# A mixture of experts after two transformer blocks: gather and output combination as two rounded passes instead of one fp32 product

## The chip, the cores and the metric

The program runs on one core of a Trainium2 chip as one launch. The metric is the device time in microseconds (us), taken from the outside. The profile comes from one execution and gives the span from the first to the last instruction, which is shorter than the device time by the launch's own ends. TensorE multiplies (PE; its weight loads are listed apart as PEld), VectorE (DVE), ScalarE (ACT) and GpSimd (POOL) work on tiles of 128 partitions, and SyncE (SP) issues most transfers from memory.

## The reference, cut to what matters

A first block of two layers (feed-forward, mixing, feed-forward on 272 tokens of 1024 features) and a second block's mixer give 256 tokens. Then comes the mixture of experts that the change is about. Each token picks one of 4 groups, in it the best 2 of 8 experts, and adds the gated outputs of both, scaled per feature by `g2`:

```python
h2 = _rms(x) * norm2_w * (1.0 + sc2) + sh2
# hier_moe: tokens are sorted to their experts, blocks of one expert each are computed, then put back
buf = jnp.zeros((n_blocks * MOE_BLOCK, d), h.dtype).at[dest].set(h[tok_sorted])
(jax.nn.silu(xb @ w1[e]) * (xb @ w3[e])) @ w2[e]
y = jax.ops.segment_sum(out[dest] * gate_sorted[:, None], tok_sorted, num_segments=n_tok)
x = x + g2 * y
```

There are 32 experts with `w1`, `w3` of 1024 x 512 and `w2` of 512 x 1024, all fp32: 6 MB each, 192 MB in all.

## The kernel before, in words

Block 1 and the mixer of block 2 (L181 to L1461) split weights and activations in a high and a low rounded part (type fp32r) and multiply them in three passes. The experts (`moe`, L1464) multiply in fp32, which the profile shows as two records for each product.

`route` (L1524) makes the router's logits, the two experts of each token, their gates and, for each expert, the place of each token among that expert's tokens. It is a chain of small operations on DVE. It also makes `h2`, the normed tokens (ACT, L1566).

Experts are worked on in 16 pairs, 64 slots for each expert, side by side on 128 columns or partitions. For a pair, or for two pairs at once, `gather` (L1641) compares places with slot numbers, which gives a 0/1 matrix `pick` of tokens x slots (L1655, DVE). The product of `h2` and `pick` (L1663, PE, in eight steps of 128 features) gives the tokens' features in the order of slots, which ACT scales and shifts into `xg` (L1664). Pair 0 and pair 15 are gathered alone; pairs 1 and 2, 3 and 4, ... 13 and 14 together, and the gather of the next two stands in the pair before them (`then`, L1725).

`pair` (L1690) multiplies `pick` with the gates (`pg`, POOL, L1699), turns it (L1704) and copies it to `pgT` (ACT, L1706). Then come the first products `ph` (L1717, w1 and w3), silu and the product of both (L1723, L1724) into the first half of the tile `y`, the turn of the result (`hTp` L1728, `hTe` L1730), and the second products `py` (L1749, w2) in two halves of 512 columns (in the last pair four pieces of 256). DVE scales each by `g2row` into `y` (L1751). `out` (L1733) multiplies `pgT` with `y` for both tiles of 128 tokens (L1736) and DVE adds the result to the tokens (`xtok`, L1737). `out` of one half follows the second products of the next.

Weights come in tiles of 1 MB, 12 a pair: 4 of w1, 4 of w3, 4 of w2. SP issues a copy for each (L1678; in the last pair in halves). They lie in a ring of 20 places that blocks 1 and 2 no longer need (L1474); a copy waits until the products with the tile 20 places earlier are done.

Before pair 7 stands a branch (`overflow`, L1507, L1513): if an expert has more than 64 tokens, a loop computes the rest. In the profiled run it isn't taken. All engines meet at the branch: each must reach it before any goes on. The copies of pair 7 are written ahead of the branch in the code (`ws[0] = iter(list(ws[0]))`, L1493), so that weights can be on their way. A scheduler orders each engine's instructions over the whole program by its own estimate of when they will be ready, and so decides which of them stand ahead of the branch.

Of the kernel before, what the change touches and what calls it, by code (L numbers as in the profile page):

```python
# [31 lines left out]
# token tiles of block 1, in the order the columns of the statistics have them:  # L32
# the first and second 128 tokens of x, then the meta tokens
# [3 lines left out]
# ---------------------------------------------------------------- constants of the shapes  # L37
# [23 lines left out]
# the partition that a rotation pairs each partition with, within 32  # L61
# [3 lines left out]
def _decay():  # L65
    """[j, h, c] = gamma_h ** (c - j) / sqrt(d) for c >= j; the tokens of a key tile are rows, the columns
    the queries from the tile's first token on"""
    f = np.float32
    lg = np.log(f(1.0) - f(2.0) ** (f(-5.0) - np.arange(HEADS, dtype=f))).astype(f)
    rel = np.arange(T, dtype=f)[None, :] - np.arange(P, dtype=f)[:, None]  # L70
    out = np.zeros((P, HEADS, T), f)
    scale = f(P ** -0.5)
    for h in range(HEADS):
        out[:, h] = np.where(rel >= 0, np.exp(lg[h] * np.maximum(rel, 0)), 0).astype(f) * scale
    return out.reshape(P, HEADS * T)
# [7 lines left out]
def _sum_matrices():  # L83
    """0/1 matrices [u, t]. For each block size, the steps u between the middle of t's block and t: forward (its
    columns t by half, the left halves' first) and backward (the right halves' first). Two levels' forward ones,
    then their backward ones; with the last level go prefixes and suffixes, for what the tile's ends are to t."""
# [21 lines left out]
def _level_masks():  # L108
    """where a pair (s, t) belongs to the block size of a level: within one block, in different halves"""
# [37 lines left out]
# the pieces that the two column halves of an expert's last product come in, within 512: of the last pair, and else  # L147
# [14 lines left out]
# columns of the feature-major parameter array: name -> (offset, columns)  # L162
# [16 lines left out]
class Kernel:  # L179
# [12 lines left out]
    # ------------------------------------------------------------------ set up  # L192
    def setup(self):
# [33 lines left out]
        # the tensor engine's clock is up when the first weights are there  # L227
# [8 lines left out]
    def rsqrt(self, out, ms):  # L236
        """out = ms ** -0.5, elementwise"""
# [4 lines left out]
    # ------------------------------------------------------------------ weights  # L242
# [5 lines left out]
    def load_first(self, *srcs):  # L248
        """the first weights of all, in pieces in the order of their use"""
# [8 lines left out]
    def split(self, part):  # L258
        """part [P, a, b] as hi + lo"""
# [16 lines left out]
    # ------------------------------------------------------------------ norms of block 1  # L276
    def norm_in(self, gname, lo, need=True):
        """xh + xl = h * g"""
# [10 lines left out]
    def norm_stats(self, lo):  # L289
        """A generator: statistics per token; needed when the first product leaves PSUM"""  # L290
# [43 lines left out]
    # ------------------------------------------------------------------ swiglu  # L334
    def ffn(self, l, nm, T0):
# [20 lines left out]
        # the first products wait in PSUM for the norm's statistics  # L356
# [45 lines left out]
    # ------------------------------------------------------------------ the mixing layer of block 1  # L402
    def mix(self, l, T0):
# [21 lines left out]
        # chains of small products, one stage of each after every projection of 128 columns  # L425
# [75 lines left out]
        def diff_head(h):  # L501
            """queries of x, in two tiles of 128: columns 0:272 and 272:416 of the scores"""
# [68 lines left out]
        def diff_meta():  # L571
            """the 16 meta tokens as queries, all heads at once"""
# [124 lines left out]
        # the values first, as they leave PSUM before the norm's statistics are there  # L697
# [27 lines left out]
        # the attention heads' half first, while the retention heads end  # L725
# [25 lines left out]
    # ------------------------------------------------------------------ block 1  # L751
# [30 lines left out]
    def tables(self):  # L782
        """what the mixing layers need besides weights"""
# [8 lines left out]
        # lambda of each layer, the same on every partition  # L792
# [19 lines left out]
    # ------------------------------------------------------------------ modulation of block 2  # L812
    def modulation(self):
        """A generator: one step of silu(c) @ w_mod + b_mod for each next()"""
# [8 lines left out]
        for part in range(6):  # L823
# [16 lines left out]
            # the sum over the partitions, as a row, by way of hi and lo  # L840
# [23 lines left out]
        # scale per feature, for the tokens (with the gain of block 1's last norm) and the context  # L864
# [6 lines left out]
        # the second norm's scale and shift; the router's weights with the scale in them, and what the shift gives  # L871
# [20 lines left out]
    def context(self):  # L892
        """A generator: the context's norm and modulation, as hi + lo"""
# [34 lines left out]
    def spread(self, rb, col):  # L928
        """rb [P, 256] = the two columns of 128 tokens each, on every partition"""
# [8 lines left out]
    def modulate(self, k, src, sc, sh, hi, lo, rb, t):  # L938
        """hi + lo = src * sc * rb + sh"""
# [6 lines left out]
    def final_stats(self):  # L946
        """rstd of block 1's last norm per token (a column per tile) and, times that of block 2's first norm,
        on every partition; the second norm's mean square comes from that of h times the first one's gain"""
# [30 lines left out]
    # ------------------------------------------------------------------ block 2  # L979
    def split_k(self, raw, kh):  # L980
        """hi and lo of half the rows of a tile of 256 columns"""
# [833 lines left out]
```

## Time and profile before

| | us |
|---|---|
| device time, median of 3 runs (lowest, highest) | 1860.05 (1859.84, 1861.5) |
| span of the profiled execution | 1856.8 |
| median less span: what lies around the span | 3.25 |
| experts' first product to the end of the span | 1335.0 to 1856.8 |
| PE busy in the span | 1794.6 (97%) |
| DVE, ACT, POOL busy | 985.9, 728.1, 356.7 |

No device time is given for the profiled execution apart from the others, so its span is set against the median. PE's busy time counts from a record's start to its modelled end, and pipelined records overlap; how often one product starts after another is read from two starts. Windows are given as busy time of each engine, the clock granted to PE (1.00 is full) and the transfers. A line number is one of the kernel before; the kernel after has other numbers (L1663 is L1674 there, L1678 is L1690, L1704 is L1717, L1717 is L1734, L1728 is L1745, L1736 is L1754, L1749 is L1767).

### The profile page before, as it was taken

The page shows a single profiled execution, that of the slowest core. Times are in us where ns is not written, and L with a number is a line of the kernel's source. Part 1 is how long each engine was busy: PE and PEld are TensorE (multiplying, and loading weights), DVE is VectorE, ACT ScalarE, POOL GpSimd, SP SyncE. Part 2 cuts the span into 40 slices and gives each one's busy share as a digit, 9 for nine tenths or more (in the row PEclk, how much of TensorE's full clock was granted, in tenths as well). Part 3 has the DMA queues.
Part 4 walks back from the last instruction along what each step waited for, and adds up shares of the span by engine and source line. Part 5 has one row for each costly group of instructions (what it writes and reads, how often), then busy time and mean ns, then how long its engine had stood idle before and what let it go on. Part 6 is the DMA issues. An engine that isn't in the chain of part 4 may idle for free. (4 is left out here: it accounts for less than half of the span.)

```text
span 1856.8 us, 29800 instructions
## 1 busy us (share of the span) xinstructions
PE 1794.6 (97%) x12083; PEld 1427.3 (77%) x12083; DVE 985.9 (53%) x1636; ACT 728.1 (39%) x1270; POOL 356.7 (19%) x373
## 2 busy tenths in 40 slices
PE   9999999999999999999999999999899998999998
PEld 8999988899999999998999998966644333433333
DVE  5875887766667677677767656375312111111112
ACT  5444444545444544445555445655311101101110
POOL 3231273221222231253131113120100000000000
PEclk9999999999999999999999999989899999999999
DMA  7766643345667577653455555424899998999991
GB/s 242 231 205 190 220 159 113 97 154 181 218 228 235 184 248 235 209 182 114 137 167 181 186 164 170 134 90 148 318 345 398 400 399 295 399 400 397 400 395 45
DMA packets 312942, 427.70 MB, mean 230 GB/s; under 512 B 15056, under 2 KB 207312, under 8 KB 312672
## 3 DMA queue, kind: packets, MB, share of 16 engines
q1 hardware_dynamic: 294640, 394.51, 61.4%
q10 hardware_dynamic: 18160, 31.23, 5.0%
q8 instruction: 98, 1.61, 0.4%
q14 instruction: 44, 0.36, 0.1%
HBM read 424.56 MB, written 1.15 MB: 229 GB/s over the span
## 5 line engine op out<-in xcount | busy, mean ns | idle before, releaser
L264 DVE TENSOR_TENSOR whl<-raw,whl 128x1024 fp32r<-128x1024 f32 (+2 forms) x374 | 465.1, 1248 | 210.7 <-ACT whl L263 209.8
L263 ACT ACTIVATE whl<-raw 128x1024 fp32r<-128x1024 f32 (+2 forms) x374 | 384.1, 1033 | 335.7 <-PE pd L274 114.2
L272 PE MATMUL pgu<-xh,whl 128*128 128x272 f32 (+1 forms) x1408 | 404.1, 287 | 2.3 <-DVE g L347 2.3
L274 PE MATMUL pgu<-xh,whl 128*128 128x272 f32 (+1 forms) x1408 | 403.4, 287 | 2.0 <-DVE whl L264 1.9
L273 PE MATMUL pgu<-xl,whl 128*128 128x272 f32 (+1 forms) x1408 | 403.3, 287 | 1.4 <-DVE xl L285 1.4
L272 PEld LDWEIGHTS pgu<-xh,whl 128*128 128x128 f32 x1408 | 264.5, 188 | 3.9 <-issue 2.2
L274 PEld LDWEIGHTS pgu<-xh,whl 128*128 128x128 f32 x1408 | 265.4, 189 | 2.6 <-DVE whl L264 2.6
L273 PEld LDWEIGHTS pgu<-xl,whl 128*128 128x128 f32 x1408 | 265.5, 189 | 2.3 <-DVE xl L285 2.1
L1717 PE MATMUL ph<-ew,xg 128*64 128x512 f32 x1024 | 237.7, 595 | 0.0
L274 PE MATMUL pd<-ah,whl 128*128 128x272 f32 (+1 forms) x704 | 203.2, 289 | 0.0
L273 PE MATMUL pd<-al,whl 128*128 128x272 f32 (+1 forms) x704 | 202.6, 288 | 0.0
L272 PE MATMUL pd<-ah,whl 128*128 128x272 f32 (+1 forms) x704 | 202.3, 287 | 0.0
L1717 PEld LDWEIGHTS ph<-ew,xg 128*64 128x64 f32 x1024 | 73.1, 137 | 143.3 <-issue 142.2
L351 POOL TENSOR_TENSOR u<-u,g 128x272 f32<-128x272 f32 (+1 forms) x88 | 92.0, 1045 | 395.1 <-DVE u L350 339.9
L1749 PE MATMUL py<-ew,hTe 128*64 128x512 f32 (+1 forms) x544 | 127.8, 572 | 11.9 <-ACT hTe L1730 6.8
L272 PE MATMUL pj<-xh,whl 128*128 128x272 f32 x448 | 133.3, 298 | 0.0
L272 PEld LDWEIGHTS pd<-ah,whl 128*128 128x128 f32 x704 | 132.9, 189 | 0.4 <-issue 0.2
L273 PEld LDWEIGHTS pd<-al,whl 128*128 128x128 f32 x704 | 132.8, 189 | 0.1
L274 PEld LDWEIGHTS pd<-ah,whl 128*128 128x128 f32 x704 | 132.6, 188 | 0.0
L273 PE MATMUL pj<-xl,whl 128*128 128x272 f32 x448 | 130.7, 292 | 0.5 <-DVE xl L285 0.5
L274 PE MATMUL pj<-xh,whl 128*128 128x272 f32 x448 | 130.3, 291 | 0.0
L1724 DVE TENSOR_TENSOR y<-y,ph 128x512 f32<-128x512 f32 x16 | 11.0, 688 | 203.2 <-PE ph L1717 203.2
(434 smaller groups left out, 2660.4 us busy)
## 6 DMA issues: line engine op xcount, KB each, us to landing
ew<-in_w_dram SPq DMA_DIRECT2D x180, 1024.0 KB, 13.8
raw<-in_ffn_w_gate_dram SPq DMA_DIRECT2D x43, 1024.0 KB, 5.6
raw<-in_ffn_w_up_dram SPq DMA_DIRECT2D x43, 1024.0 KB, 5.3
raw<-in_w_in_dram SPq DMA_DIRECT2D x38, 1024.0 KB, 5.0
raw<-in_ffn_w_down_dram SPq DMA_DIRECT2D x32, 1024.0 KB, 5.8
mraw<-in_w_mod_dram ACTq DMA_DIRECT2D x24, 1024.0 KB, 5.6
raw<-in_ffn_w_down_dram SPq DMA_DIRECT2D x16, 768.0 KB, 5.7
ew<-in_w_dram SPq DMA_DIRECT2D x24, 512.0 KB, 10.3
```

Of the source, the lines that this page charges most:

```text
L263: nc.scalar.activation(w[:, 0], part, AF.Copy)
L264: nc.vector.tensor_tensor(w[:, 1], part, w[:, 0].bitcast(F32), op=ALU.subtract)
L272: nc.tensor.matmul(out, wh, xh, start=first, stop=False)
L273: nc.tensor.matmul(out, wh, xl, start=False, stop=False)
L274: nc.tensor.matmul(out, wl, xh, start=False, stop=last)
L351: nc.gpsimd.tensor_tensor(u[:, :N], u[:, :N], g[:, :N], op=ALU.mult)
L1717: nc.tensor.matmul(ps[half(j)], xg[4 * kk + k][:, half(j)], w[j][:, k], start=kk + k == 0, stop=kk == 1 and k == 3)
L1724: nc.vector.tensor_tensor(h, h, ph[1], op=ALU.mult)
L1749: nc.tensor.matmul(py[half(j), n, c], hT[:, k, half(j)], w[j][:, k, c], start=k == 0, stop=k == 3)
```

## The change

The gather and the output combination multiply by a matrix of zeros and ones in type fp32r, once with the high part of the other factor and once with its low part, and add both. For this the gates leave the matrix: `pgT` is now the turned `pick` itself, and a product of `pg` with a column of ones (L1719) gives each slot's gate as a column `gs`, which scales `y` on DVE. `h2` becomes `h2h` (ACT) and `h2l` (DVE), `y` becomes `yh` (ACT) and `yl` (DVE). `h2l` lies at the place "gb" and the pool of three further places loses one, so the ring of weight places has 18.

```diff
-                         + one(self.xq, "rec", "qs", "xlo", "att") + [raw] * 2 + [whl] * 4 + one(self.gp, "gb")
-                         + one(self.mw, "e0", "e1", "e2"))
+                         + one(self.xq, "rec", "qs", "xlo", "att") + [raw] * 2 + [whl] * 4
+                         + one(self.mw, "e0", "e1"))
...
-        self.h2 = self.gp.tile([P, 2, D], F32, name="h2", tag="ga")
+        self.h2h = self.gp.tile([P, 2, D], F32R, name="h2h", tag="ga")
+        self.h2l = self.gp.tile([P, 2, D], F32R, name="h2l", tag="gb")
...
-            nc.scalar.activation(self.h2[:, tt], self.xtok[:, tt], AF.Copy, scale=r)
+            for b2 in range(2):
+                bs_ = slice(b2 * 512, b2 * 512 + 512)
+                nc.scalar.activation(self.h2h[:, tt, bs_], self.xtok[:, tt, bs_], AF.Copy, scale=r)
+        def h2_low():
+            for tt in range(2):
+                nc.vector.scalar_tensor_tensor(self.h2l[:, tt], self.xtok[:, tt], ss[:, tt, 4:5],
+                                               self.h2h[:, tt].bitcast(F32), op0=ALU.mult, op1=ALU.subtract)
...
         self.place = ep.tile([P, 2, 32], F32, name="place")
+        h2_low()
...
-        pick = sm.tile([P, 2, n], F32, name="pick", tag="pick", bufs=1)
+        pick = sm.tile([P, 2, n], F32R, name="pick", tag="pick", bufs=1)
...
-            for tt in range(2):
-                nc.tensor.matmul(ps[:, :n], self.h2[:, tt, ks], pick[:, tt], start=tt == 0, stop=tt == 1)
+            for i in range(4):
+                nc.tensor.matmul(ps[:, :n], (self.h2h, self.h2l)[i % 2][:, i // 2, ks], pick[:, i // 2],
+                                 start=i == 0, stop=i == 3)
...
-            nc.tensor.transpose(pt[:, tt * P:(tt + 1) * P], pg[:, tt], self.ident)
-        pgT = self.late.tile([P, SEQ], F32, name="pgT", tag="pgT", bufs=1)
+            nc.tensor.transpose(pt[:, tt * P:(tt + 1) * P], pf[:, tt], self.ident)
+        for tt in range(2):
+            nc.tensor.matmul(pt[:, SEQ:SEQ + 1], pg[:, tt], self.ones[:, 0:1], start=tt == 0, stop=tt == 1)
+        pgT = self.late.tile([P, SEQ], F32R, name="pgT", tag="pgT", bufs=1)
         nc.scalar.activation(pgT, pt[:, :SEQ], AF.Copy)
+        gs = self.late.tile([P, 1], F32, name="gs", tag="gs", bufs=1)
+        nc.scalar.activation(gs, pt[:, SEQ:SEQ + 1], AF.Copy)
...
-        y = self.late.tile([P, D], F32, name="y", tag="y", bufs=1)
-        h = y[:, :512]
+        h = self.late.tile([P, 512], F32, name="h", tag="y", bufs=1)
+        yh = self.late.tile([P, D], F32R, name="yh", tag="yh", bufs=1)
+        yl = self.late.tile([P, D], F32R, name="yl", tag="yl", bufs=1)
...
-                nc.tensor.matmul(po, pgT[:, tt * P:(tt + 1) * P], y[:, ns], start=True, stop=True)
+                for i, w in enumerate((yh, yl)):
+                    nc.tensor.matmul(po, pgT[:, tt * P:(tt + 1) * P], w[:, ns], start=i == 0, stop=i == 1)
...
-                nc.vector.tensor_tensor(y[:, ns], py[:, n, c], self.g2row[:, ns], op=ALU.mult)
+                y = self.late.tile([P, 512], F32, name="y", tag="y", bufs=1)[:, c]
+                nc.vector.scalar_tensor_tensor(y, py[:, n, c], gs, self.g2row[:, ns], op0=ALU.mult, op1=ALU.mult)
+                nc.scalar.activation(yh[:, ns], y, AF.Copy)
+                nc.vector.tensor_tensor(yl[:, ns], y, yh[:, ns].bitcast(F32), op=ALU.subtract)
```

What else changes is where a scratch tile of the router lies (`xq`, now under the name "yl"), and comments, which are gone.

The change also moves instructions. SP's queue in front of the branch, before: the last ten copies of pair 7 (`ew` is a weight tile, `in_w1_2` and so on the weights it comes from, `mi` the number that the branch reads).

```order
L1678 DMA ew_15554<-in_w1_2_dram 128x4x512
L1678 DMA ew_15557<-in_w3_2_dram 128x4x512
L1678 DMA ew_15558<-in_w3_2_dram 128x4x512
L1678 DMA ew_15561<-in_w3_2_dram 128x4x512
L1678 DMA ew_15562<-in_w3_2_dram 128x4x512
L1678 DMA ew_15565<-in_w2_2_dram 128x4x512
L1678 DMA ew_15566<-in_w2_2_dram 128x4x512
L1678 DMA ew_15569<-in_w2_2_dram 128x4x512
L1678 DMA ew_15570<-in_w2_2_dram 128x4x512
L1513 TENSOR_LOAD mi_14651
L1513 COMPARE_AND_BRANCH
```

All twelve copies of pair 7 are issued ahead of the branch. SP's queue in front of the branch now: the last copies of pair 6 and the first three of pair 7.

```order
L1690 DMA ew_15683<-in_w2_2_dram 128x4x512
L1690 DMA ew_15698<-in_w2_2_dram 128x4x512
L1690 DMA ew_15699<-in_w2_2_dram 128x4x512
L1690 DMA ew_15730<-in_w1_2_dram 128x4x512
L1690 DMA ew_15731<-in_w1_2_dram 128x4x512
L1690 DMA ew_15734<-in_w1_2_dram 128x4x512
L1513 COMPARE_AND_BRANCH
```

The branch has come ahead of the rest of pair 7. SP's queue from the end of the branch on now:

```order
L1690 DMA ew_15735<-in_w1_2_dram 128x4x512
L1690 DMA ew_15738<-in_w3_2_dram 128x4x512
L1690 DMA ew_15739<-in_w3_2_dram 128x4x512
L1690 DMA ew_15742<-in_w3_2_dram 128x4x512
L1690 DMA ew_15743<-in_w3_2_dram 128x4x512
L1690 DMA ew_15746<-in_w2_2_dram 128x4x512
L1690 DMA ew_15747<-in_w2_2_dram 128x4x512
L1690 DMA ew_15750<-in_w2_2_dram 128x4x512
L1690 DMA ew_15751<-in_w2_2_dram 128x4x512
L1690 DMA ew_16485<-in_w1_2_dram 128x4x512
```

Nine copies of pair 7 have moved behind the branch, and the number that it reads is fetched earlier, ahead of what is shown.

PE, the output products of an early pair among the first products `ph` of the next, before:

```order
L1749 MATMUL py<-ew,hTe 64x512 x8
L1704 MATMUL pgt<-ident,pg 128x128 x2
L1717 MATMUL ph_15093<-ew,xg 64x512 x2
L1749 MATMUL py<-ew,hTe 64x512 x8
L1736 MATMUL po<-y,pgT 128x512 x4
L1717 MATMUL ph_15093<-ew,xg 64x512 x13
```

The output products of both halves stand together behind the second half of `py`. The same place in an early pair now (`pick` is turned in place of `pg`, and `pgt<-ones,pg` makes the column of gates):

```order
L1717 MATMUL pgt<-ident,pick 128x128 x2
L1719 MATMUL pgt<-ones,pg 128x1 x2
L1734 MATMUL ph_15023<-ew,xg 64x512 x2
L1767 MATMUL py<-ew,hTe 64x512 x8
L1754 MATMUL po<-yh,pgT 128x512
L1754 MATMUL po<-yl,pgT 128x512
L1754 MATMUL po<-yh,pgT 128x512
L1754 MATMUL po<-yl,pgT 128x512
L1734 MATMUL ph_15023<-ew,xg 64x512 x2
L1754 MATMUL po<-yh,pgT 128x512
L1734 MATMUL ph_15023<-ew,xg 64x512 x2
L1754 MATMUL po<-yl,pgT 128x512
```

Four output products have become eight, and first products of the next pair stand between those of the second half. In pair 5 they do not:

```order
L1767 MATMUL py<-ew,hTe 64x512 x7
L1754 MATMUL po<-yl,pgT 128x512
L1734 MATMUL ph_15496<-ew,xg 64x512
L1754 MATMUL po<-yh,pgT 128x512 x2
L1754 MATMUL po<-yl,pgT 128x512 x2
L1734 MATMUL ph_15496<-ew,xg 64x512 x15
```

Here one first product lies between the last second product and the output products of the second half.

DVE in the route, now (`r` are the router's small tiles, `L` the logits, `ss` the means of squares):

```order
L1590 TENSOR_TENSOR r_14598<-L,r_14596 128x8
L1573 SCALAR_TENSOR_TENSOR h2l<-xtok,ss_14575,h2h 128x1024
L1591 TENSOR_TENSOR r_14598<-r_14598,cst 128x8
L1599 TENSOR_TENSOR r_14605<-L,r_14604 128x64
L1592 TENSOR_REDUCE r_14597<-r_14598 128x2
L1573 SCALAR_TENSOR_TENSOR h2l<-xtok,ss_14575,h2h 128x1024
L1593 TENSOR_TENSOR r_14598<-r_14598,r_14597 128x8
```

Both subtractions stand early in the chain that ends in the picks, though the code calls them behind the places.

## Rows read from the trace of the kernel before

**Rows 1.** Page, part 2: the span in 40 equal slices.

```profile
PE   9999999999999999999999999999899998999998
...
GB/s 242 231 205 190 220 159 113 97 154 181 218 228 235 184 248 235 209 182 114 137 167 181 186 164 170 134 90 148 318 345 398 400 399 295 399 400 397 400 395 45
```

**Rows 2.** Windows: us; busy (count) PE, PEld, DVE, ACT, POOL; PEclk, DMA, GB/s.

```profile
1300.00:1350.00 50.00, 44.54 (x222) 30.60 (x222) 17.68 (x58) 16.03 (x28) 5.96 (x9) 0.90 0.87 318
...
1549.00:1556.50 7.50, 4.84 (x16) 1.38 (x12) 2.08 (x4) 0.00 (x0) 0.00 (x0) 1.00 0.01 4
1556.50:1565.00 8.50, 6.86 (x30) 5.20 (x31) 0.76 (x2) 3.54 (x7) 0.87 (x2) 1.00 0.81 265
1600.00:1650.00 50.00, 48.41 (x212) 19.35 (x210) 6.97 (x11) 6.99 (x13) 1.51 (x4) 1.00 1.05 398
...
1814.00:1857.00 43.00, 36.16 (x171) 14.57 (x170) 9.20 (x18) 1.58 (x3) 0.00 (x0) 1.00 0.08 26
```

**Rows 3.** The weight tiles `ew`: who uses them, idle time by releaser.

```profile
L1717 PE MATMUL ph<-ew,xg x1024: 592/592/644, 1335.0 to 1835.0; 128*64 128x512 f32 x171
...
L1678 SPq DMA_DIRECT2D ew<-in_w_dram x204: 367/2394/4582, 1171.1 to 1806.7; - x102
...
  DMA ew<-in_w_dram: 0.6, 3
```

**Rows 4.** Chain of waits in the experts' stage: start us, us, what.

```profile
1590.63 3.82 PE po L1736 x8
...
1606.61 7.29 PE xgp L1663 x32
...
1667.97 7.30 PE xgp L1663 x32
...
1717.28 0.68 DVE y L1751
...
1748.46 0.70 DVE y L1751
...
1821.68 13.91 PE ph L1717 x64
1835.59 0.03 issue
```

**Rows 5.** Waits of SP's queue, 1530 to 1560: us, times, longest.

```profile
SPq L1513 <- SPq L1513: 10.7, 3, 5.3
SPq L1678 <- PEq L1513: 6.7, 1, 6.7
```

**Rows 6.** Timeline around the branch: start us, us, engine, line, operation.

```profile
1556.88 1.95 SPq L1678 DMA_DIRECT2D ew<-in_w_dram  x2
1556.94 0.76 DVE L1655 TENSOR_TENSOR pick<-place,cst 128x256 f32<-128x256 f32 x2 [1.59 <-PEq L1513]
```

**Rows 7.** Timeline in the mixer: rounded products of 256 columns.

```profile
1149.83 0.28 PE L998 MATMUL tok<-whl,xhi 128*128 128x256 f32 x1
1149.83 0.19 PEld L996 LDWEIGHTS tok<-whl,xhi 128*128 128x128 f32 x1
1149.94 0.28 PE L996 MATMUL tok<-whl,xhi 128*128 128x256 f32 x1
```

**Rows 8.** Timeline in the mixer: rounded products of 512 columns.

```profile
1299.86 0.39 PE L1435 MATMUL out<-whl,yh 128*128 128x512 f32 x1
...
1300.09 0.40 PE L1436 MATMUL out<-whl,yl 128*128 128x512 f32 x1
```

**Rows 9.** Lines by form, 1290 to 1857: count, busy us, mean ns; idle before.

```profile
L1664 ACT ACTIVATE xg<-xgp,m2col 128x256 f32<-128x256 f32 x56 | 31.5, 564 | 77.8 <-PE xgp L1663 71.5 <-PE ph L1717 6.3
...
L1751 DVE TENSOR_TENSOR y<-py,g2row 128x512 f32<-128x512 f32 x30 | 20.7, 692 | 170.8 <-PE py L1749 162.1 <-PE ph L1717 8.7
...
L1723 ACT ACTIVATE y<-ph 128x512 f32<-128x512 f32 x16 | 9.6, 597 | 95.6 <-PE ph L1717 95.6
...
L264 DVE TENSOR_TENSOR whl<-raw,whl 128x1024 fp32r<-128x1024 f32 x4 | 4.7, 1222 | 4.6 <-ACT whl L263 4.6
```

**Rows 10.** Timeline in the route: the router's products.

```profile
1319.68 1.08 PE L1544 MATMUL lg<-wr,x2T 128*128 128x36 f32 x8
```

More of the change, by code (lines that the diff above doesn't have):

```diff
@@ L1547, in route @@
         for b2 in range(2):
-            t = sm.tile([P, 512], F32, name="xq", tag="pick", bufs=1)
+            t = self.late.tile([P, 512], F32, name="xq", tag="yl", bufs=1)
             nc.scalar.activation(t, self.xtok[:, 0, b2 * 512:b2 * 512 + 512], AF.Square, accum_out=ss[:, 0, b2:b2 + 1])
@@ L1697, in pair @@
         pg = self.late.tile([P, 2, P], F32, name="pg", tag="pg", bufs=1)
+        pf = pick.bitcast(F32)
         for tt in range(2):
             nc.gpsimd.tensor_tensor(pg[:, tt].rearrange("p (e s) -> p e s", s=CAP),
-                                    pick[:, tt].rearrange("p (e s) -> p e s", s=CAP),
+                                    pf[:, tt].rearrange("p (e s) -> p e s", s=CAP),
                                     gate[:, tt, :, None].to_broadcast([P, 2, CAP]), op=ALU.mult)
```

## The prediction, made before the kernel was run

> **What bounds the kernel now.** I read the page's 40 slices first: PE is at 9 tenths almost throughout and the transfer rate stands at 395 to 400 GB/s from slice 31 on, with one dip to 295 in slice 34 [rows 1]. So two candidates stand in the experts' stage (from 1335 us [rows 3] to the end), and the windows over it put numbers on them: PE 48.4 busy of 50 us, DMA at 398 GB/s with a share of 1.05, which I take as full [rows 2]. Who waits for whom decides. Of all 1024 first-product records the weight loads waited for a transfer three times, 0.6 us together; the last weight copy is issued at 1806.7 [rows 3], and after 1814 the rate is 26 GB/s [rows 2], while work goes on for 43 us. So PE sets the end and the loads run ahead of it. The chain of waits agrees: it is PE's products, with short DVE waits (0.68 to 0.70 us) where y leaves PSUM [rows 4].
>
> The dip is the branch. SP issues nothing there: 6.7 us of its queue's wait end with PE's arrival at L1513 [rows 5]. In 1549 to 1556.5 the core moves 4 GB/s, then 265 [rows 2]; the next weight copy is issued at 1556.88 and DVE goes on at 1556.94 [rows 6]. I call that moment B: 1556.9 before, 300 us before the end. The 96 tiles of 1 MB that are loaded behind it arrive by 1814, in 257 us: at 398 GB/s one takes 1.0486/0.398 = 2.635 us, 95 of them 250.3, and 6.8 are left for the first.
>
> **The change, part by part, up to the branch (7 pairs).**
> Output product. Before: 4 products of 512 columns as 8 records, 3.82 us a pair [rows 4]. Now 8 rounded products, each starting 0.23 us after the one ahead (1299.86 to 1300.09) [rows 8]: 1.86, with switches of tile shape some 2.3, so 1.5 saved (1.1 to 1.96). Seven pairs: -10.5.
>
> Gather of two pairs. Before 32 records, 7.30 us [rows 4]. Now 32 rounded products of 256 columns at 0.11 to 0.12 us (1149.83 to 1149.94 [rows 7]), 3.7 on PE. But each of the 8 results leaves through ACT in 0.564 [rows 9], and only two banks take turns: 8 x 0.564 and 0.6 for hTe queued behind make 5.1. Saved 2.2 to 3.6; I take 2.4, for ACT's row is of this very instruction. Three groups: -7.2. The single-pair gathers have 32 narrow records before and after, and I count nothing (0 to 1.5).
>
> Here a rule weighs against the change. Each rounded product brings a load of 128 columns of 0.19 us, and the products still start 0.11 to 0.12 us apart [rows 7], so loads lie beside products. The Trainium skill says (TensorE: Matmul & The Clock Gate, section "The mechanism") that "LDWEIGHTS overlaps with in-flight MATMULs only when row_grp differs"; all rows here use the whole array, and the trace does not agree. It is a rival below.
>
> Column of gate sums. Two more products of one column and one ACT copy. Nearest is the router's 8 records of 36 columns in 1.08 us [rows 10], 0.135 each: 4 records 0.5 a pair (0.2 if loads are hidden). +3.5.
>
> Conversions. y is now followed by a rounding on ACT (the 512-wide ACT row is 0.597) and a subtraction on DVE (0.692) [rows 9], 1.3 us more before the last output product may start. In five pairs PE's order has first products in between, as shown above, and they hide it; ahead of them 0.7 of y alone was exposed. In pairs 5 and 6 one first product or none lies between: +1.5. What waits is PE's output product at the head of its queue, and behind it the next pair's first products; on DVE the adds into xtok (L1737) stand behind the subtraction, and nothing but the end of the kernel waits for them. In front of the branch the last drain is 0.9 longer.
>
> Route. Two DVE subtractions 1024 wide now stand in the chain of small operations that makes the picks; the nearest row is L264, 1.222 us [rows 9]: +2.4 (0 if ACT's half is late anyway and slack takes them; 3 if they wait for it). The clock granted averages 0.90 in 1300 to 1350 [rows 2]; PE idling 2.4 us longer may hold it down a little: +1.0.
>
> Sum: -10.5 - 7.2 + 3.5 + 1.5 + 0.9 + 2.4 + 1.0 = -8.4. B moves to 1548.5. From the bounds (output 1.1 to 1.96, gather 2.2 to 3.6, columns 0.2 to 0.5, route 0 to 4) B lies in 1542 to 1553.
>
> **Behind the branch (9 pairs) the bound changes.** The ring goes from 20 places to 18, and what matters more is where SP's copies stand: before, all 12 of pair 7 are issued ahead of the branch, now 3. The other 9 join the 96 behind it: 105 tiles, and no transfer during the wait for PE, which hid them before. The last lands at B + 6.8 + 104 x 2.635 = B + 281, where it was B + 257. What lies beside it on PE: 300 less 9 x 1.5 (output) less 4 x 2.4 (gathers) plus 9 x 0.5 (columns), plus 6 for conversions not covered in most pairs and 0.9 of the last drain, is 288. Both are now near each other, and the tail decides. The last four tiles come in the last 10.5 us; the pair's first products, 13.9 us for eight tiles [rows 4], can end 1.8 us after their last tile, at T - 8.7, and from their end (1835.6) to the span's the kernel took 21.2. So the end is T + 12.5 = B + 293.5, 5 us later than PE alone would allow. Span: 1548.5 + 293.5 = 1842.0.
>
> The span before is 1856.8, the median of the runs 1860.05; I add the difference, 3.3: **1845 us**, 15 less (0.8%).
>
> **A page's bandwidth.** The rate in full windows is 398 GB/s [rows 2]. The Trainium skill (DMA: Bandwidth & Descriptors, section "Where 436 GB/s comes from") has about 358 GB/s per core as what binds a load from HBM; the trace does not agree. By that figure a tile takes 2.93 us, the last lands 31 us later, and my estimate from that page would be 1876.
>
> **Rivals.**
> 1. The moved copies are hidden and PE stays the bound: end at B + 288, 1840. For it: transfers had up to 43 us in hand at the end [rows 2]. Against: nine tiles take 24 of it back, PE's saving 12 more, and the tail needs the rest. 0.18.
> 2. Slower. Every output half pays the conversions in full: 1.3 us more, twice a pair, since PE's order of a later stage leaves nothing between the last of py and po. Before the branch 14 x 1.3 = 18.2 in place of 1.5: B = 1565; behind it 18 x 1.3 = 23.4 in place of 6: 305.6. Span 1871, time 1874. By PE alone the sign turns from about 0.9 us a half on (9.9 and 18 saved before and behind the branch without any such wait, over 32 halves). For it: the waits for y that the chain shows now (0.68, 0.70 [rows 4]) grow to exactly this where nothing stands between. Against: five of the first seven pairs have records between. 0.10.
> 3. PE saves less and starves early: B at its upper bound, 1553; behind it 294, with 1.1 saved per output and 0.3 more of waits a pair; and 4 to 8 on top, since in pairs 7 and 8 the first products reach their tiles before these land (nine of pair 7's twelve are not there at B) and a PE that is no faster than the loads doesn't make it up. 1854 to 1858. For it: the loads need 12 x 2.635 = 31.6 a pair, which PE alone would need as well (288/9 = 32.0). 0.14.
> 4. Weight loads are not hidden beside rounded products: 0.19 + 0.12 each, a gather of 9.9 instead of 7.3, and the output 8 x (0.19 + 0.23) = 3.4 instead of 3.8. Against the forecast that is 5.0 more in each of three gathers and 1.1 in each of seven pairs, B = 1571, and behind it 288 + 4 x 5.0 + 9 x 1.1 = 318: 1892. Against it: [rows 7]. 0.02. It is what the page quoted on weight loads would have.
> The change does what it says: the products shown above are split in the order, so "no effect" is no rival.
>
> **How the numbers follow.** Forecast, 1837 to 1853 by B's bounds and a rate between 395 and 400 GB/s: 0.56. Rival 1 (1833 to 1843): 0.18. Rival 3: 0.14, half of it above 1856.3. Rivals 2 and 4: 0.12. A change of 0.2% (3.7 us) is about what a measurement here can tell from none. Faster by more, below 1856.3: 0.56 + 0.18 + 0.07 = 0.81. Within: 0.07 and 0.01 of rival 2 in a weaker form: 0.08. Slower: 0.11. The range 1832 to 1857 leaves out rivals 2 and 4 and a tail at each side.
>
> **What would show it.** In the new profile: output products 1.9 to 2.3 us a pair; gathers about 5 us with ACT as releaser; the branch near 1548, SP's wait there longer than 6.7 us, and before it a stretch without transfers of more than 7.5 us; then 398 to 400 GB/s until about 1830 and weight loads of the first and second products waiting for transfers, which were 0.6 us. If they wait for nothing, rival 1 holds. If PE waits for DVE yl over 0.9 us twice a pair, rival 2. The forecast is wrong if B lies above 1553 or if the end comes less than 288 us after it.

## The result: slower, 1872.24 us

The changed kernel takes 1872.24 us, the median of 4 runs (1870.85 to 1878.12); the kernel before took 1859.94 beside it (1858.23 to 1861.5). The ratio is 1.0075, interval 1.0056 to 1.0094: slower, by 0.75% or 14 us (12.3 by the medians), where 1845 was forecast. The profiled execution took 1871.92, with a span of 1870.3, 13.5 more than before.

First the page, part 2, of the kernel after, in 40 slices [rows 1]:

```profile
PE   9999999999999999999999999999899987989988
PEclk9999999999999999999999999989899998999999
GB/s 241 228 208 197 222 162 92 113 161 169 232 224 229 201 209 263 200 155 113 152 165 180 192 172 156 158 46 193 270 382 397 397 367 366 397 397 385 373 359 23
```

PE has more slices at 7 and 8 tenths behind slice 32 than before, and the clock row has an 8 in slice 34. The dip of the transfers in slice 34 has become two shallow ones, in 33 and 34. Windows of the same trace put numbers on it (columns as in [rows 2]):

```profile
1550.00:1600.00 50.00, 38.33 (x167) 17.27 (x169) 9.64 (x16) 8.16 (x17) 2.43 (x6) 0.90 1.00 367
1600.00:1650.00 50.00, 47.57 (x212) 18.29 (x208) 6.83 (x10) 8.01 (x16) 0.76 (x2) 1.00 1.05 398
1660.00:1670.00 10.00, 7.96 (x26) 2.59 (x23) 2.73 (x4) 1.07 (x3) 0.00 (x0) 0.83 1.05 408
...
1750.00:1800.00 50.00, 45.33 (x191) 17.00 (x190) 12.10 (x19) 7.66 (x17) 1.51 (x4) 0.98 1.02 376
1800.00:1850.00 50.00, 47.71 (x204) 19.36 (x201) 6.65 (x10) 7.03 (x15) 0.00 (x0) 0.92 0.44 153
```

In 1600 to 1650 the clock is that of before and PE's busy time 0.8 us less. Time is lost at the branch (first row: 38 of 50 us busy) and in stretches where the granted clock falls to the half level, 1.2 GHz.

Next the weight tiles: who uses them, and the idle time of PE and of its weight loads by releaser [rows 3].

```profile
L1734 PE MATMUL ph<-ew,xg x1024: 592/592/1112, 1338.3 to 1848.4; 128*64 128x512 f32 x171
...
L1690 SPq DMA_DIRECT2D ew<-in_w_dram x204: 367/506/4686, 1171.7 to 1816.0; - x102
...
  DMA ew<-in_w_dram: 0.6, 2
```

SP's wait at PE's branch, between 1480 and 1600 (us, times, longest) [rows 5]:

```profile
SPq L1690 <- PEq L1513: 11.3, 1, 11.3
```

That wait stands before the first copy of pair 8. The nine copies behind SP's branch are issued long before it (SP, between 1531 and 1547: start, us):

```profile
1531.41 15.30 SPq L1690 DMA_DIRECT2D ew<-in_w_dram  x9
```

The compare instruction of the branch, on SP and on PE (its queue is listed as PEld): durations in ns, then the start:

```profile
L1513 SPq COMPARE_BRANCH  x1: 50/50/50, 1519.4 to 1519.4; - x1
L1513 PEldq COMPARE_BRANCH  x1: 5961/5961/5961, 1552.0 to 1552.0; - x1
```

The same two in the kernel before:

```profile
L1513 SPq COMPARE_BRANCH  x1: 50/50/50, 1538.4 to 1538.4; - x1
L1513 PEldq COMPARE_BRANCH  x1: 3501/3501/3501, 1553.2 to 1553.2; - x1
```

The weight loads of the first products waited for a transfer twice, 0.6 us in all, as before: the transfers do not bound. SP is through its branch at 1531.4, some 27 us ahead of PE (1557.9), and issues the nine copies that stand behind it while PE is still at pair 6. So the order in which the copies stand in the program says nothing of when they start. The description of the kernel before has it that all engines meet at the branch. They do not: there too SP compares 15 us ahead of PE. The 10.7 us in [rows 5] are SP's own way through the branch, and the 6.7 us are the wait of one copy, the 97th tile and the first of pair 8, in both kernels. In the code the loop of `overflow` may use the ring's places other than the last twelve (`self.ring[:-12]`), which would hold back that copy and not those of pair 7; no run tested this.

PE's groups of the kernel after between 1330 and 1875 (count, busy us, mean ns, idle before by releaser):

```profile
L1734 PE MATMUL ph<-ew,xg 128*64 128x512 f32 x1024 | 250.8, 606 | 0.0
...
L1674 PE MATMUL xgp<-pick,h2h 128*128 128x256 f32 x112 | 31.7, 315 | 10.9 <-DVE pick L1666 6.6 <-ACT xg L1676 2.7 <-DVE xtok L1755 1.6
...
L1754 PE MATMUL po<-yh,pgT 128*128 128x512 f32 x60 | 23.6, 447 | 9.3 <-ACT yh L1771 9.0
```

The same view of the kernel before:

```profile
L1717 PE MATMUL ph<-ew,xg 128*64 128x512 f32 x1024 | 237.7, 595 | 0.0
...
L1736 PE MATMUL po<-y,pgT 128*128 128x512 f32 x120 | 58.9, 619 | 3.1 <-DVE y L1751 3.1
L1663 PE MATMUL xgp<-pick,h 128*128 128x256 f32 x224 | 52.5, 390 | 4.2 <-DVE pick L1655 2.9 <-ACT xg L1664 0.7 <-issue 0.6
```

Output products of 512 columns wait 9.3 us, nearly all for the conversion, where they waited 3.1 for y. The 1024 first products, which the change doesn't touch, became longer.

**Where the time went.** I added up PE's records of the experts' stage from the trace: a record's work is the time to the next record's start less any wait, and half of the work in stretches at the half clock is put apart as lost to the clock (us).

| | before | after | change |
|---|---|---|---|
| gather products | 59.4 | 40.3 | -19.1 |
| output products | 61.7 | 41.8 | -19.9 |
| column of gate sums, transposes of it | 5.9 | 11.4 | +5.5 |
| first and second products, hTp | 365.8 | 383.6 | +17.8 |
| PE's waits | 24.3 | 37.2 | +12.9 |
| the branch | 2.9 | 6.6 | +3.7 |
| half clock | 1.7 | 11.8 | +10.1 |
| stage | 521.8 | 532.7 | +10.9 |

The stage is taken from PE's first gather product to its last record. It also starts 2.4 later. The rounded products gave what was expected of them: -33.5 with the columns. Everything else took it back, and more.

### The profile page after: what moved, and what is told of

The parts are those of the page before. It is cut to its first block, busy times and chain, and to the rows that moved or that the text cites. A ratio compares the mean times of both kernels' runs of the same rounds, so it can differ in the third digit from the quotient of the medians.

```text
span 1870.3 us, 30016 instructions
## 1 busy us (share of the span) xinstructions
PE 1785.6 (95%) x12147; PEld 1427.8 (76%) x12147; DVE 1008.4 (54%) x1672; ACT 747.0 (40%) x1322; POOL 359.3 (19%) x373
## 5 line engine op out<-in xcount | busy, mean ns | idle before, releaser
L1734 PE MATMUL ph<-ew,xg 128*64 128x512 f32 x1024 | 250.8, 606 | 0.0
L1767 PE MATMUL py<-ew,hTe 128*64 128x512 f32 (+1 forms) x544 | 140.8, 581 | 13.6 <-DVE y L1770 7.4
L1741 DVE TENSOR_TENSOR h<-h,ph 128x512 f32<-128x512 f32 x16 | 11.0, 688 | 221.7 <-PE ph L1734 221.7
```

What stands on the lines that cost most here:

```text
L1734: nc.tensor.matmul(ps[half(j)], xg[4 * kk + k][:, half(j)], w[j][:, k], start=kk + k == 0, stop=kk == 1 and k == 3)
L1741: nc.vector.tensor_tensor(h, h, ph[1], op=ALU.mult)
L1767: nc.tensor.matmul(py[half(j), n, c], hT[:, k, half(j)], w[j][:, k, c], start=k == 0, stop=k == 3)
```

## Experiments

Each is told against the kernel before, run beside it. The ring of weight tiles has 20 places in the kernel before and 18 in the changed one.

**1. The kernel before with 18 places.**

```diff
-  ... + [whl] * 4 + one(self.gp, "gb") + one(self.mw, "e0", "e1", "e2"))
+  ... + [whl] * 4 + one(self.mw, "e0", "e1"))
```

> The kernel before with 18 ring places in place of 20 and nothing else. In the order SP's branch then stands behind 87 weight copies instead of 96, as in the kernel after. Theory: nine copies go out while PE still works ahead of the branch, their transfers run until PE's branch instruction has fetched what follows it, and that takes about 6 us instead of 3.5; PE then idles over 6 us, the granted clock falls to half for some 10 us, and the time is 4 to 6 us longer: 1864 to 1866. Rival (the loads are late behind the branch, the prediction's mechanism): first products wait for weights, and the time is 5 or more us longer without a longer branch. Rival (the ring does not matter): 1859 to 1861, branch 3.5 us.

Measured: 1875.88 us against 1858.32, ratio 1.0079 (1.0054 to 1.0103). Two places fewer cost 17.6 us by the medians, 10 to 19 by the ratio, with the fp32 products as they were; the expectation of 4 to 6 was too small. Its trace has for the weight tiles (idle time of PE and of its loads together by releaser, us and times):

```profile
  DVE y L1751: 24.2, 30
  ACT hTe L1730: 23.3, 28
...
  DMA ew<-in_w_dram: 0.3, 1
```

And for the window behind the branch:

```profile
1550.00:1600.00 50.00, 40.94 (x156) 17.23 (x152) 6.88 (x12) 5.98 (x11) 2.38 (x6) 0.93 0.95 353
```

No load is waited for (0.3 us). What moved is PE's order behind the branch, here a piece of it:

```
+L1728 MATMUL hTp<-ident,y 128x128 x4
+L1749 MATMUL py<-ew,hTe 64x512
+L1704 MATMUL pgt<-ident,pg 128x128 x2
+L1749 MATMUL py<-ew,hTe 64x512 x8
+L1736 MATMUL po<-y,pgT 128x512 x2
+L1749 MATMUL py<-ew,hTe 64x512 x7
 L1717 MATMUL ph_16171<-ew,xg 64x512
-L1728 MATMUL hTp<-ident,y 128x128 x4
-L1717 MATMUL ph_16171<-ew,xg 64x512 x2
-L1749 MATMUL py<-ew,hTe 64x512 x8
-L1704 MATMUL pgt<-ident,pg 128x128 x2
-L1717 MATMUL ph_16171<-ew,xg 64x512 x2
-L1749 MATMUL py<-ew,hTe 64x512 x8
-L1736 MATMUL po<-y,pgT 128x512 x4
-L1717 MATMUL ph_16171<-ew,xg 64x512 x11
+L1736 MATMUL po<-y,pgT 128x512 x2
```

Rows with a minus are the order before: the next pair's first products (`ph_16171`) stand between the turn hTp and the second products py, between the two halves of py, and in numbers behind the output products. With 18 places (plus) one of these records is left, between the last second product and the last output products.

By the account of the table, behind the branch: work +5.3, waits +7.1, half clock +2.9, branch +2.4. Against this kernel with as many places the changed one can't be told apart: its ratio is 1.0075, this one's 1.0079, and either lies in the other's interval.

**2 and 3. One product rounded, the other as before.** In experiment 2 the output product is the old one, and in 3 the gather; 19 places in both, which is what their tiles leave room for.

```diff
# experiment 2, against the changed kernel
-  for i, w in enumerate((yh, yl)):
-      nc.tensor.matmul(po, pgT[:, tt * P:(tt + 1) * P], w[:, ns], start=i == 0, stop=i == 1)
+  nc.tensor.matmul(po, pgT[:, tt * P:(tt + 1) * P], y[:, ns], start=True, stop=True)
# experiment 3
-  for i in range(4):
-      nc.tensor.matmul(ps[:, :n], (self.h2h, self.h2l)[i % 2][:, i // 2, ks], pick[:, i // 2], ...)
+  for tt in range(2):
+      nc.tensor.matmul(ps[:, :n], self.h2[:, tt, ks], pick[:, tt].bitcast(F32), ...)
```

> The kernel before with the gather alone in two rounded passes (19 ring places; SP's branch stands behind 87 copies). Theory: gathers save 2 us per two pairs and pair 15 nothing, 14 in all; the route costs 2.4; the branch with transfers beside it and the slow clock behind it cost 4 to 6; no slow clock later, since there are no conversions to wait for: 1851 to 1855. Rival (gathers paced by ACT leave PE idle enough for the clock to fall): stretches at half clock beside gathers, 1858 to 1864.

> The kernel before with the output combination alone in two rounded passes (19 ring places; SP's branch stands behind 96 copies, as before). Theory: output products save 1.2 us a pair (19), the gate column costs 0.5 (8), conversions 0.6 a pair (10), and where PE waits for yh twice within a few us the clock falls (3 to 5); the branch is as short as before: 1860 to 1864. Rival 2 of the prediction (conversions in full at every half): 1872 or more. Rival (the slow clock comes from the branch alone): no stretch at half clock after 1340, 1856 to 1860.

Measured: 1866.43 (ratio 1.0036, 1.0022 to 1.005) and 1864.42 (1.0027, 1.0014 to 1.004), against 1858.32. Neither half alone wins. The expectation of 3 nearly holds. That of 2 missed by 11 us; it had left out the growth of the second products, 7.9 us. What one place less costs isn't shown in either. They do separate the growth of the untouched products: the second products take 130.3 us in 2 and 122.7 in 3 (before 122.4, after 130.8), the first products 232.0 in 2 and 240.1 in 3 (before 233.5, after 242.3). The one growth comes with the rounded gather, the other with the rounded output.

**4. A shorter conversion.** The scaling by g2 leaves the pairs: yh goes from PSUM by ACT with the gate as scale, yl from PSUM by DVE, and the sums gather in a tile of their own (17 places are left).

```diff
-  nc.vector.scalar_tensor_tensor(y, py[:, n, c], gs, self.g2row[:, ns], op0=ALU.mult, op1=ALU.mult)
-  nc.scalar.activation(yh[:, ns], y, AF.Copy)
+  nc.scalar.activation(yh[:, ns], py[:, n, c], AF.Copy, scale=gs)
...
```

> The kernel after with y's scaling by g2 taken out of the pairs: yh is written by ACT from PSUM with the gate as its scale, yl by DVE from PSUM, outputs add up in a tile of their own (a ring place less, 17), and that tile times g2 is added to the tokens in the last pair. Theory: PE waits 0.65 for yh instead of 1.4, the stretches at half clock at pairs 9 and 13 go (3.4 us), waits shrink by some 6; the long branch stays: 1861 to 1865. Rival (the clock falls because of the branch and the gathers alone): waits shrink, the stretches stay, 1866 to 1869.

Measured: 1866.21, ratio 1.0043 (1.003 to 1.0056). By the ratios that is 6 us better than the changed kernel, a little less than expected. The longest wait of an output product falls from 1.5 to 0.9 us, but there are 16 of them in place of 7, 10.0 us together in both; the half-clock stretches from the branch on fall from four to two.

**5. The changed kernel with the cover put back.** Cover is what PE's order puts between a conversion's start and the product that waits for it. A fixed place in PE's order: the second half's output products stand behind eight records of the next pair's first products. The ring stays at 18.

```diff
+  if self.pending and not i and not kk and k == 1:
+      with self.tc.issue_after(last.ins):
+          self.flush()
...
-  out(due.pop(0))
+  self.pending.append(lambda: out(due.pop(0)))
...
```

> The kernel after, with the output products of a pair's second half put, by a fixed edge on PE, behind the first eight first products of the next pair (pgT gets a second buffer). Nothing else: 18 places, SP's branch behind 87 copies as in the kernel after. Theory (PE's order leaves conversions uncovered behind the branch, and the clock falls after the waits): the wait for yh behind the second half (1.4 us in some ten pairs) and the stretches at half clock at pairs 9 and 13 go: 12 to 16 us less, 1856 to 1860; the long branch stays. Rival (waits only move to other places, since ACT and DVE are late as before): 1868 to 1872.

Measured: 1855.77 against 1858.77, ratio 0.9981 (0.9971 to 0.9991), some 16 us better than the changed kernel by an edit to the order alone (for it `pgT` gets a second buffer), as expected. PE's line for the output products, between 1330 and 1875:

```profile
L1761 PE MATMUL po<-yh,pgT 128*128 128x512 f32 x60 | 25.0, 447 | 1.5 <-ACT yh L1778 1.5
```

Its windows:

```profile
1650.00:1700.00 50.00, 48.25 (x214) 19.27 (x214) 12.35 (x19) 8.39 (x18) 1.56 (x4) 1.00 1.05 398
1750.00:1800.00 50.00, 47.44 (x200) 16.87 (x202) 11.35 (x19) 5.01 (x11) 1.49 (x4) 1.00 1.05 397
1800.00:1850.00 50.00, 45.56 (x230) 20.60 (x226) 11.62 (x23) 8.16 (x18) 0.00 (x0) 1.00 0.43 153
```

The idle time before the output products fell from 9.3 to 1.5 us and the clock is whole in all three windows. From the branch on the stage takes 297.4 us in place of 314.6: waits -7.9, work -5.2, half clock -4.1. The branch is as long as in the changed kernel.

**6. Experiments 4 and 5 together.** The diff is that of both; 17 places.

> The edits of the last two together: outputs added up in a tile of their own and scaled by g2 at the end (17 places), and the second half's output products behind eight first products of the next pair. Theory: 4 to 6 us less than with the order alone, since the first half's yh also comes 0.75 us earlier: 1851 to 1856, which would be under the kernel before. Rival (the first half is covered by the second products anyway): same as with the order alone.

Measured: 1852.89 against 1858.77, ratio 0.9973 (0.9961 to 0.9985): faster than both kernels, by 6 and 19 us. Against experiment 5 it is 2.9 us, less than the 4 to 6 expected, and the two intervals overlap.

**7 and 8. The changed kernel, and the one before, without the branch.** Both leave out the loop for tokens beyond the 64 places of an expert.

```diff
-  self.overflow(names)
```

> The kernel after without the branch and the loop for tokens beyond 64 slots. Theory: the 6.6 us of PE's wait at the branch, 1.8 us of slow clock behind it and 1 us of drain go: 1861 to 1864; the uncovered conversions stay. Rival (the branch only shows a wait for weights): weight waits in its place, 1868 to 1872.

> The kernel before without the branch and the loop. Theory: the 2.9 us of PE's wait and about 1 us of drain go, no clock to win: 1854 to 1857, so that the branch explains about 5 us of the difference between the two kernels. Rival (order behind the branch depends on the branch): the order of PE changes and the time is longer.

Measured: 1866.79 (ratio 1.0041, 1.0029 to 1.0053) and 1868.31 (1.0062, 1.0043 to 1.0082), against 1858.77. The first is 3 us above what was expected. The second is the surprise: the kernel before loses 10 us when its branch goes. Its 20 places are untouched; PE's order in pairs 7 to 15 becomes the uncovered one, and its waits are 31.4 us in place of 24.3. That is the rival of its expectation. Over the whole stage its waits grow by 7 us and its work by 6, about as in experiment 1 (8 and 5). From pair 7 on PE's records stand in the same order in both, by kind, from the first to the last. So this order costs some 13 us, whichever edit brings it about; the rest of experiment 1's cost is its branch and its clock, 5 us by the account above. Without the branch the changed kernel's clock still falls four times behind 1344, so the branch is not what lowers it there.

**9. The kernel before with 18 places and the edge of experiment 5.** The fp32 products stay.

> The kernel before with 18 places (1875.9 alone) and the same edge on PE as in the run with late output products: those of a pair's second half stand behind the first four first products of the next pair (eight records). fp32 products as before. Theory: the order recovers about 5 to 9 us of the 17 that 18 places cost, since the wait for y (0.7 us) is all that it covers here: 1866 to 1871; against the kernel after with the same edge (1855.8) that leaves 10 to 15 us for the rounded products. Rival (the rounded products are worth nothing on the chip): the same time as the kernel after with the edge, 1854 to 1858.

Measured: 1873.57 against 1858.95, ratio 1.008 (1.0063 to 1.0097), 2.3 below experiment 1 by the medians and not at all by the ratios; the expectation was too hopeful. The edge covers the output product alone, whose wait behind the branch falls from 3.6 to 0.5 us; the second products' waits (12.7 us, 8.8 before) stay. With the same ring and the same edge, rounded products against fp32 ones is experiment 5 against 9: 1855.8 to 1873.6, 17.8 us in favour of the rounded ones.

**10. All of pair 7's copies written behind the branch** (one run, without an interval).

```diff
-  ws[0] = iter(list(ws[0]))
```

> The kernel after with all twelve copies of pair 7 written behind the branch, so that none of them is under way when PE crosses it. Theory: PE's branch instruction takes 3.5 us as in the kernel before, not 6, for no weights are in flight beside it; pair 7 then waits for weights some 8 us. Rival (the branch is longer since its code is larger or lies elsewhere): 6 us again. The time by itself tells little: 1866 to 1880.

Measured: 1874.04. The scheduler still puts 87 tiles ahead of SP's branch, as in the changed kernel. But only one more goes out before PE is through its own, in place of nine, and 104 follow. With that the weight loads of first and second products wait 2.7 us for transfers, in 9 places, where 8 us were expected. Windows of 3.5 us in PE's branch, first of the kernel before:

```profile
1553.20:1556.70 3.50, 1.43 (x4) 0.36 (x2) 1.38 (x2) 0.00 (x0) 0.00 (x0) 1.00 0.02 7
```

The changed kernel:

```profile
1553.20:1556.70 3.50, 0.00 (x0) 0.00 (x0) 0.00 (x0) 0.00 (x0) 0.00 (x0) 0.50 1.05 407
```

This one:

```profile
1553.80:1557.30 3.50, 0.11 (x1) 0.00 (x0) 1.19 (x2) 0.00 (x0) 0.00 (x0) 0.59 0.03 7
```

And the line on its weight tiles:

```profile
  DMA ew<-in_w_dram: 2.7, 9
```

PE's branch instruction takes 3.50 us in the first, 5.96 in the second and 3.56 here: it is short where the transfers stand still (7 GB/s) and long where they run (407).

**11. PE kept busy where it waits.** Eight rounded products of 256 columns ahead of the second half's output products, from pair 5 on; their result is overwritten.

```diff
+  if self.g >= 5 and not end and ns.start == 512 and not tt:
+      for _ in range(8):
+          nc.tensor.matmul(po[:, :SEQ], self.ones_r, pgT, start=True, stop=True)
```

> The kernel after with eight rounded products of 256 columns, whose result is overwritten, in front of the output products of the second half from pair 5 on (0.94 us each time, in a wait of 1.4). Theory (the clock falls after idle PE): the three stretches at half clock at pairs 9, 13 and 14 become fewer, the products cost nothing where PE waited: 1864 to 1870. Rival (the clock does not depend on these waits): the stretches stay and the time is the same or up to 8 us longer.

Measured: 1875.5, ratio 1.0096 (1.008 to 1.0113): no faster than the changed kernel, whose interval it overlaps, and not the 1864 to 1870 expected. Yet its windows show the clock that was hoped for:

```profile
1650.00:1700.00 50.00, 45.70 (x200) 18.70 (x199) 9.73 (x15) 8.03 (x16) 1.56 (x4) 1.00 1.02 383
1750.00:1800.00 50.00, 46.24 (x209) 18.98 (x206) 10.05 (x16) 8.04 (x16) 1.51 (x4) 1.00 1.02 376
1800.00:1850.00 50.00, 48.02 (x223) 20.32 (x222) 8.69 (x13) 8.09 (x18) 0.00 (x0) 1.00 0.56 199
```

The clock is whole where it was 0.98 and 0.92, the half clock costs 2.4 us behind the branch in place of 8.3, and the waits are 4 shorter; the filling itself adds 11.0 us of work there. So it is PE's waits that let the clock fall behind the branch, and products that do nothing are no cheaper than the fall.

## Why the prediction was wrong

**Output and gathers: right.** Forecast 10.5 and 13.5 for the output, 7.2 and 9.6 for the gathers, 40.8 together; measured 19.9 for the output and 19.1 for the gathers, 39.0. The output saved 4.1 less and the gathers 2.3 more than forecast, so the sum fits better than its parts. The columns: forecast 8 us, measured 7.1, less 1.6 on the transposes. Loads lie beside rounded products: the gather's records stand 0.12 us apart, with a load of 0.19 beside each, so rival 4 doesn't hold here. From the timeline of after:

```profile
1564.33 0.28 PE L1674 MATMUL xgp<-pick,h2l 128*128 128x256 f32 x1
1564.33 0.19 PEld L1674 LDWEIGHTS xgp<-pick,h2h 128*128 128x128 f32 x1
1564.45 0.28 PE L1674 MATMUL xgp<-pick,h2h 128*128 128x256 f32 x1
```

The sentence that the prediction quotes from the Trainium skill (TensorE: Matmul & The Clock Gate, "The mechanism") has loads beside products only where their row groups (row_grp) differ. This trace does not agree with it. The same section also names a background weight buffer that a load may go to ahead of time, and no run here shows which of the two is at work.

**Route: about right.** The two subtractions take 1.27 us each, and the stage starts 2.4 later, the forecast's number. The exact agreement is luck: the profiles of the five kernels with the old route start their first gather at 1328 to 1333 and the eight with the new one at 1333 to 1339, 4.5 later on average.

**Conversions: too small behind the branch.** Forecast 2.4 us ahead of it, measured +3.3; behind it 6.9, measured +9.6. About half of that (4.9) is at output products, four of which wait 1.5 us each where nothing stands between; 2.9 are at gathers. The timeline of after shows one such place (start, us, engine, operation, idle before):

```profile
1660.53 0.75 DVE L1770 SCALAR_TENSOR_TENSOR y<-py,gs,g2row 128x512 f32<-128x512 f32 x1 [2.53 <-PE ph L1734]
1661.31 0.63 ACT L1771 ACTIVATE yh<-y 128x512 fp32r<-128x512 f32 x1 [5.99 <-DVE y L1770]
...
1661.99 0.73 PE L1754 MATMUL po<-yh,pgT 128*128 128x512 f32 x2 [1.50 <-ACT yh L1771]
...
1664.03 0.39 PE L1674 MATMUL xgp<-pick,h2h 128*128 128x256 f32 x1 [0.54 <-DVE xtok L1755]
...
1664.58 5.34 PE L1734 MATMUL ph<-ew,xg 128*64 128x512 f32 x14
```

PE waits 1.50 and 0.54 us within 4, and then 14 first-product records take 5.34 us where 16 take 3.65 elsewhere: the half clock. The forecast looked for what stands between in the order of the first seven pairs and let it hold for the last nine. There the order is another one.

**B, the moment when PE is through the branch: forecast 1548.5, measured 1557.9.** It lies above 1553, the bound that was to make the forecast wrong. Of the 9.4 us, 5.1 are the first and second products and hTp ahead of the branch, for which nothing was counted, 2.5 the longer branch instruction, 2.3 a smaller saving in the output; the rest nearly cancels.

**The copies behind the branch: the step that failed by its mechanism.** "The other 9 join the 96 behind it ... and no transfer during the wait for PE" took SP to pass the branch when PE does. SP was through alone 27 us sooner, the transfers ran at 407 GB/s in PE's branch, and loads were waited for 0.6 us, 2.7 even in experiment 10. [rows 5] already had SP's way through the branch apart from its wait for PE. There was no tail to wait for.

**Behind the branch by PE alone: forecast 288, measured 312.4.** This sum carries the error in size: the tail of loads had added only 5 us to it. Not counted: first and second products +12.6, half clock +8.3, the rest of the longer branch 1.2; conversions 2.7 more than forecast. The ring was weighed by its copies only. What it does, experiment 1 shows for the kernel before: 17.6 us with the loads in time, which its trace puts down to PE's order, the clock and the branch.

**Rivals.** Rival 2's time, 1874, is 2 from the result, and a part of its mechanism came true: PE's order behind the branch leaves nothing between the last py and po. But that struck six halves of 32, four of them behind the branch, and output products waited 6.4 us more (10.0 against 3.6), not the 41 that it adds up to; so the near hit is luck. Rival 1's premise (copies hidden, PE the bound) holds; its time (1840) doesn't. That the ring changes PE's order, and with it the clock, was in no rival.

So the cause, as far as shown: the rounded arithmetic saves 33 us and its conversions need cover; taking two places from the ring costs 17.6 us by itself (experiment 1), most of it PE's order, which costs about as much in experiment 8 with all 20 places; with cover put back by hand the change wins (5 and 6). Three things stay open. The first and second products keep their growth in experiments 5 and 6, and only a part of it is explained below. With fp32 products the cover of the output alone brings nothing that is clear of noise (9), so which gap in the order costs the ring's time there isn't shown. And the changed kernel with 20 places wasn't tried, since its tiles leave no room for them. The spread of the stage's start among kernels with the same route, some 5 us, isn't explained either, so the stage is compared from its first gather on.

## What to carry to other kernels

When a change takes buffers from a pool, compare the scheduled order of the other engines stage by stage before pricing the arithmetic: a wait costs nothing only where the order puts other work in it, and the order of one stage doesn't hold for the next. A saving on the bounding engine that lengthens the chain between two of its steps needs its cover written into the order, as experiment 5 did. And ask of a branch which engines pass it early.

## What the runs showed of the hardware

- PE's branch instruction, with the loop not run, takes 3.5 to 3.6 us with transfers at 7 GB/s (before, experiment 10) and 5.3 to 6.3 with weight transfers at 163 to 403 GB/s (after and experiments 1 to 6, 9, 11). SP gets through the same branch 27 us ahead of PE in the changed kernel.
- The granted clock falls to 1.2 GHz in a kernel whose PE is busy 95% of the span: at 1552.1, as PE reaches the branch 1.4 us after a wait of 1.51, and later behind waits such as those at 1661.99 and 1664.03. Behind the branch this costs 8.3 us. Not every such wait is followed by a fall: those of 1.5 us at 1596 and 1729 are not, while in experiment 7 those at 1594 and 1727 are; and the fall at 1818 has only a wait of 0.55 ahead of it. Experiments 5 and 11 remove the later stretches by covering or filling the waits.
- Products on half of the array's columns run two at a time: a pair starts within 0.05 us and takes 0.42 us to the next start. Where a whole-array product stands between, one runs alone, with 0.52 to the next start, as in the timeline of after:

```profile
1603.45 0.59 PE L1734 MATMUL ph<-ew,xg 128*64 128x512 f32 x1
1603.97 0.39 PE L1674 MATMUL xgp<-pick,h2l 128*128 128x256 f32 x1
1604.29 3.65 PE L1734 MATMUL ph<-ew,xg 128*64 128x512 f32 x16
```

In the changed kernel 14 records of first products stand right before an output product and take 0.56 us each to its start, 7.9 us in all. In the kernel before and in experiment 2 none does; in experiment 3 there are 21, with 11.0 us. So the growth of the first products, which came with the rounded output, is mostly these broken pairs. It does not explain the second products: of first and second products together 728 start within 0.05 us of the next record before, 694 after and 698 in experiment 3, where the second products did not grow. Why they grow with the rounded gather is not shown.
